# The last row blocks of a matmul with RMS norm: a square for VectorE, a product and scalings for GpSimd

## The chip, the cores and the metric

The kernel runs on one core of a Trainium2 chip. A core has five engines with a queue each: TensorE (PE in the profile), which multiplies matrices into PSUM; VectorE (DVE); ScalarE (ACT); GpSimd (POOL); and SyncE (SP), which here issues the output DMAs. The time is the device time of one execution in microseconds, the median over several runs.

## The reference

```python
def setup_inputs():
    m, k, n = 2048, 2048, 2048
...
def reference(a, b, gamma, eps):
    x = np.matmul(a, b)
    rms = np.sqrt(np.mean(x ** 2, axis=-1, keepdims=True) + eps)
    return (gamma * x / rms).astype(np.float32)
```

Each row of the product is divided by its root mean square over 2048 columns, and multiplied by gamma column by column. All arrays are float32.

## The kernel before

The 2048 rows are done in 16 row blocks of 128 rows, and the columns in four chunks of 512 (`CH`). After a first part that multiplies plainly, row blocks go in pairs (`ra`, `rb`), and each pair of row blocks with each half of the columns is one 2x2 block product. It is computed with seven products instead of eight, in the manner of Strassen and Winograd (`do(n, m)` runs product m of segment n); for some segments the same is done once more on a larger scale (`step`). Partial results lie in PSUM banks (`B1`, `B2`, `B3`, `B7`, `tbank`) and in SBUF tiles `x11`, `x12`, `x21`, `x22`; the helper `add` (L101) joins them on VectorE, and ScalarE copies banks.

Behind each row block come the norm and the output. ScalarE squares a piece and sums it along the row into one column of `msq` (`square_of`, L272, whose squared values go to a junk tile `sq`). A ScalarE root (`root`, L288) of the sums, with the rest of the sum as bias, gives the root mean square, VectorE's reciprocal (L293) gives the row's factor, and the rows are multiplied by it and by gamma and written out by DMAs that SyncE issues. The junk tile comes from a pool with a single buffer (`sq_pool`, bufs=1), and every square asks that pool for its tile anew.

The order of the work on each engine is the order of the program text; nothing reorders it (`manual_schedule`). Waits between engines follow from which tile an operation reads or writes. SyncE's queue also runs in program order: a DMA that waits for its tile holds up those behind it.

The change lies in `last_group`, which finishes row blocks 14 (`ra`) and 15 (`rb`), at the end of the kernel. What matters there, in order of the text:

- `r_a`, the factor of row block 14, is ready. Its four chunks are scaled: `left` by ScalarE (`by_r`, L754), `mid` by GpSimd (L820), `x11[1]` by VectorE (L822; this chunk was multiplied by gamma earlier), `x12[1]` by VectorE with factor and gamma at once (`scaled_gamma`, L750). Three DMAs take them out (L819, L821, L827).
- In between, VectorE adds `x21[1]` to the two half banks (`half`) and to `x22[1]`, which is the last chunk but one of row block 15 to be complete.
- `do(n, 4)` completes `b2[0]`, chunk 0 of row block 15. ScalarE squares `b2[0]` and `x22[1]`; VectorE multiplies chunk 0 by gamma into `xb` and sums what is known of the row's squares (`pre_b`, L832).
- TensorE ends with eight matmuls on each of two half banks of 256 columns (L839), which are chunk 2 of row block 15. ScalarE squares each half (L842). Behind the first, VectorE adds its sum to the rest (`part`) and multiplies `x22[1]` by gamma into `chunk[3]`.
- Root and reciprocal give `r_b`. VectorE scales chunk 0 (L848), and a 256 KB DMA takes it out (L849); ScalarE scales chunks 1 and 3, which lie in the tile `wide`, VectorE the two halves of chunk 2 with gamma, and a DMA of 768 KB takes out the three chunks (L854).

Of the kernel before, what the change touches and what calls it, by code (L numbers as in the profile page):

```python
# [8 lines left out]
FP32 = mybir.dt.float32  # L9
BF16 = mybir.dt.bfloat16  # L10
# [3 lines left out]
ALU = mybir.AluOpType  # L14
# [3 lines left out]
def kernel(  # L18
# [13 lines left out]
    nc = tc.nc  # L32
    P = 128
# [6 lines left out]
    CH = 512  # L40
# [12 lines left out]
    sq_pool = ctx.enter_context(tc.tile_pool(name="sq_pool", bufs=1))  # L53
# [4 lines left out]
    inv_sqrt_n = 1.0 / float(N) ** 0.5  # L58
# [41 lines left out]
    def add(out, in0, in1, op=ALU.add):  # L100
        nc.vector.tensor_tensor(out=out, in0=in0, in1=in1, op=op)  # L101
# [104 lines left out]
    msq = {}  # L206
# [53 lines left out]
    def x_tile(mb, h):  # L260
        if (mb, h) not in x_half:
            x_half[mb, h] = x_slot[slot_of[mb, h]]
        return x_half[mb, h]

    def x_chunk(mb, c):
        return x_tile(mb, c // 2)[:, (c % 2) * CH:(c % 2 + 1) * CH]

    def square_of(mb, src):
        c = n_sq[mb]
        n_sq[mb] += 1  # L270
        sq = sq_pool.tile([P, 2 * CH], BF16, name="sq")
        nc.scalar.activation(out=sq[:, 0:src.shape[-1]], in_=src, func=ACTF.Square,  # L272
                             scale=inv_sqrt_n, accum_out=msq[mb][:, c:c + 1])

    def square_half(mb, h):
        square_of(mb, x_tile(mb, h))
# [4 lines left out]
    def take_pre(mb):  # L281

        pre_of[mb] = stat_pool.tile([P, 1], FP32, name="pre")
        add(pre_of[mb], msq[mb][:, 0:1], msq[mb][:, 1:2])
# [11 lines left out]
    def square_right(mb):  # L296

        square_half(mb, 1)
        rms_of[mb] = root(msq[mb][:, 2:3], pre_of.pop(mb))

    def rows(mb, lo, hi):
        return out[mb * P:(mb + 1) * P, lo:hi]
# [207 lines left out]
    x11, x12, x21, x22 = (x_chunk(r, c) for r in (r2, r3) for c in (2, 3))  # L510
# [45 lines left out]
    def chunks(n):  # L556
        g, j = halves[n]
        return [x_chunk(2 * g + r, 2 * j + c) for r in range(2) for c in range(2)]

    def do(n, m, copies=True):  # L560

        if n >= len(halves) or n < 0:
            return
        g, j = halves[n]
        b1, b2, b3 = B1[n % 2], B2[n % 2], B3[n % 2]
        if g >= G2:
            b1 = b2
        product(g, j, m, {1: b1, 2: b1, 3: b3, 4: b2, 5: b3, 6: b2, 7: B7}[m],
                start=m in (1, 7))
        if m == 1 and g >= G2:  # L570
            nc.scalar.copy(out=chunks(n)[0], in_=b2)
        elif m == 1:
            nc.scalar.copy(out=b2, in_=b1)  # L573
        elif m == 6:
            nc.scalar.copy(out=b3, in_=b2)  # L575
        elif m == 7 and copies:
            nc.scalar.copy(out=chunks(n)[2], in_=B7)  # L577
# [44 lines left out]
    def first_sums(n):  # L622

        return [chunks(m)[0] for m in (n - 2, n - 1, n, n + 1)]
# [115 lines left out]
    def last_group():  # L740
        n = len(halves) - 2
        g = NG - 1
        ra, rb = 2 * g, 2 * g + 1
        x11, x12, x21, x22 = zip(chunks(n), chunks(n + 1))
        xa, xb = x_tile(ra, 0), x_tile(rb, 0)
        gam = [gamma_sb[:, c * CH:(c + 1) * CH] for c in range(NCH)]
        gam_left = gamma_sb[:, 0:HALF]

        def scaled_gamma(x, src, r, gamma_of_x):
            nc.vector.scalar_tensor_tensor(out=x, in0=src, scalar=r, in1=gamma_of_x,  # L750
                                           op0=ALU.mult, op1=ALU.mult)

        def by_r(x, r):
            nc.scalar.activation(out=x, in_=x, func=ACTF.Copy, scale=r)  # L754

        b2, b3 = [B2[(n + j) % 2] for j in range(2)], [B3[(n + j) % 2] for j in range(2)]
        x00, x01 = first_sums(n)[0:2]
        do(n, 6)
        step(g - 1, 1, X2)
        nc.scalar.copy(out=W2, in_=X2)  # L760
        square_right(rb - 2)
        do(n - 1, 3)
        step(g - 1, 2, W2)
        step(g - 1, 6, X2)
        nc.scalar.copy(out=Y2, in_=X2)
        finish(rb - 2)
        take(n - 1, 12)
        add(x00, W2, x00)
        do(n + 1, 1)
        step(g - 1, 5, Y2)  # L770
        step(g - 1, 7, W2)
        step(g - 1, 4, X2)
        square_half(ra - 2, 0)
        add(x11[1], Y2, x11[1])
        a_sums(g, (4,))
        add(x11[0], W2, x11[0])
        add(x11[1], W2, x11[1])
        take_pre(ra - 2)
        square_of(ra, x11[1])
        do(n, 5)  # L780
        nc.scalar.copy(out=x22[0], in_=b3[0])
        add(x11[0], X2, x11[0])
        step(g - 1, 3, Y2)
        add(x01, Y2, x01)
        square_right(ra - 2)
        do(n + 1, 6)
        finish(ra - 2)
        do(n, 7)
        add(x22[0], x21[0], x22[0])
        add(b2[0], b2[0], x21[0])  # L790
        square_of(rb, x22[0])
        add(x11[1], x11[1], gam[2], ALU.mult)
        do(n + 1, 5)
        nc.scalar.copy(out=x22[1], in_=b3[1])
        wide = a_pool.tile([P, K], FP32, name="a32")
        chunk = [wide[:, c * CH:(c + 1) * CH] for c in range(NCH)]
        add(chunk[1], x22[0], gam[1], ALU.mult)
        pre_b = stat_pool.tile([P, 1], FP32, name="part")
        add(pre_b, msq[rb][:, 0:1], msq[rb][:, 1:2])
        do(n, 3)  # L800
        take(n, 12)
        square_half(ra, 0)
        pre_a = stat_pool.tile([P, 1], FP32, name="pre")
        nc.vector.tensor_scalar(out=pre_a, in0=msq[ra][:, 0:1], scalar1=msq[ra][:, 1:2],
                                scalar2=msq[ra][:, 2:3], op0=ALU.add, op1=ALU.add)
        add(xa, xa, gam_left, ALU.mult)
        do(n + 1, 3)
        take(n + 1, 12)
        square_of(ra, x12[1])
        rms_a = root(msq[ra][:, 3:4], pre_a)  # L810
        r_a = inverse(rms_a)
        other = X2
        product(g, 1, 7, other)
        nc.scalar.copy(out=x21[1], in_=other)
        halves2 = [slice(0, CH // 2), slice(CH // 2, CH)]
        half = [bank[:, 0:CH // 2] for bank in (B1[1], b3[0])]
        left, mid = xa[:, 0:CH], xa[:, CH:]
        by_r(left, r_a)
        nc.sync.dma_start(out=rows(ra, 0, CH), in_=left)  # L819
        nc.gpsimd.tensor_scalar_mul(out=mid, in0=mid, scalar1=r_a)  # L820
        nc.sync.dma_start(out=rows(ra, CH, HALF), in_=mid)  # L821
        nc.vector.tensor_scalar_mul(out=x11[1], in0=x11[1], scalar1=r_a)  # L822
        for bank, col in zip(half, halves2):
            add(bank, b2[1][:, col], x21[1][:, col])
        add(x22[1], x21[1], x22[1])
        scaled_gamma(x12[1], x12[1], r_a, gam[3])
        nc.sync.dma_start(out=rows(ra, HALF, N), in_=x_tile(ra, 1))  # L827
        do(n, 4)
        square_of(rb, b2[0])
        square_of(rb, x22[1])  # L830
        add(xb[:, 0:CH], b2[0], gam[0], ALU.mult)
        nc.vector.tensor_scalar(out=pre_b, in0=pre_b, scalar1=msq[rb][:, 2:3],  # L832
                                scalar2=msq[rb][:, 3:4], op0=ALU.add, op1=ALU.add)

        half_sq = stat_pool.tile([P, 2], FP32, name="n2")
        part = stat_pool.tile([P, 1], FP32, name="part")
        for h, (bank, col) in enumerate(zip(half, halves2)):
            for kp in range(KP):
                nc.tensor.matmul(bank, quarter(g, 1, 1)[:, kp, :], sums[1][:, 2, kp, col],  # L839
                                 start=False, stop=(kp == KP - 1), skip_group_check=True)  # L840
            sq = sq_pool.tile([P, 2 * CH], BF16, name="sq")
            nc.scalar.activation(out=sq[:, 0:CH // 2], in_=bank, func=ACTF.Square,  # L842
                                 scale=inv_sqrt_n, accum_out=half_sq[:, h:h + 1])
            if h == 0:
                add(part, half_sq[:, 0:1], pre_b)
                add(chunk[3], x22[1], gam[3], ALU.mult)
        r_b = inverse(root(half_sq[:, 1:2], part))
        nc.vector.tensor_scalar_mul(out=xb[:, 0:CH], in0=xb[:, 0:CH], scalar1=r_b)  # L848
        nc.sync.dma_start(out=rows(rb, 0, CH), in_=xb[:, 0:CH])  # L849
        for c in (1, 3):  # L850
            by_r(chunk[c], r_b)
        for bank, col in zip(half, halves2):
            scaled_gamma(chunk[2][:, col], bank, r_b, gam[2][:, col])
        nc.sync.dma_start(out=rows(rb, CH, N), in_=wide[:, CH:])  # L854

    first_segment()
# [37 lines left out]
```

## Time and profile before

| | |
|---|---|
| median of 3 runs | 219.91 us (219.65 to 221.15) |
| the profiled execution's own time | 219.88 us |
| its span, first to last instruction | 218.1 us |
| TensorE matmul busy | 207.6 us (95%), granted clock 0.991 |
| VectorE busy | 161.9 us (74%) |
| ScalarE busy | 113.6 us (52%) |
| GpSimd busy | 36.8 us (17%), of it one computation in the last 50 us |
| SyncE: output DMAs | 32 |

In the profile a line is that of the kernel, L12 being line 12; where a helper such as `add` records every operation, all of them show the helper's line, and the tile names tell them apart. Lines of a timeline give the start in us from the span's start, the duration, the engine, the line, the operation, its output and inputs with their shapes, and in brackets how long the engine was idle before it and what released it. SPq is SyncE's queue of DMAs. Ends of matmuls are modelled, and durations on GpSimd are rough.

### The profile page before, as it was taken

The page shows a single profiled execution, that of the slowest core. Times are in us where ns is not written, and L with a number is a line of the kernel's source. Part 1 is how long each engine was busy: PE and PEld are TensorE (multiplying, and loading weights), DVE is VectorE, ACT ScalarE, POOL GpSimd, SP SyncE. Part 2 cuts the span into 40 slices and gives each one's busy share as a digit, 9 for nine tenths or more (in the row PEclk, how much of TensorE's full clock was granted, in tenths as well). Part 3 has the DMA queues.
Part 4 walks back from the last instruction along what each step waited for, and adds up shares of the span by engine and source line. Part 5 has one row for each costly group of instructions (what it writes and reads, how often), then busy time and mean ns, then how long its engine had stood idle before and what let it go on. Part 6 is the DMA issues. An engine that isn't in the chain of part 4 may idle for free.

```text
span 218.1 us, 2969 instructions
## 1 busy us (share of the span) xinstructions
PE 207.6 (95%) x1004; PEld 97.1 (45%) x1024; DVE 161.9 (74%) x327; ACT 113.6 (52%) x225; POOL 36.8 (17%) x73
## 2 busy tenths in 40 slices
PE   7899999999999999999999999999999999999970
PEld 3444544444455444444444444444444444444440
DVE  1128769999999974989985899399856984485781
ACT  2110002900598565889726962594728951555782
POOL 7544444334001000300021001100101000000030
PEclk9999999999999999999999999999999999999996
DMA  7999999999949888599774995497595993040454
GB/s 153 171 201 207 203 206 209 212 207 221 408 171 377 304 228 238 150 345 283 237 227 168 345 277 100 183 243 241 126 273 215 316 256 72 0 192 3 192 187 198
DMA packets 37039, 46.60 MB, mean 214 GB/s; under 512 B 22560, under 2 KB 26656, under 8 KB 35744
## 3 DMA queue, kind: packets, MB, share of 16 engines
q0 software_dynamic: 10608, 23.86, 45.3%
q1 hardware_dynamic: 26144, 22.29, 34.8%
q10 hardware_dynamic: 272, 0.26, 0.3%
q8 instruction: 8, 0.13, 0.2%
q14 instruction: 7, 0.06, 0.1%
HBM read 34.60 MB, written 16.78 MB: 236 GB/s over the span
## 4 chain that ended last, share of the span: by engine, by line
PE 80%; DMA 6%; ACT 6%; DVE 4%; issue 2%; POOL 1%; ACTq 0%; another core or an unknown queue 0%; SPq 0%; POOLq 0%
PE acc L358 53%; PE acc L406 16%; PE acc L397 3%; DMA early<-in_a_dram 3%; DMA out_dram<-x 3%; ACT sq L272 2%; PE tbank L397 2%; PE tbank L432 2%; DVE x L311 2%; PE tbank L182 2%; PE tbank L358 1%; DVE x L101 1%; ACT acc L573 0%; PE tbank L195 0%; POOL b L115 0%
## 5 line engine op out<-in xcount | busy, mean ns | idle before, releaser
L358 PEld LDWEIGHTS <-s 128*128 128x128 f16 (+1 forms) x312 | 30.4, 98 | 37.5 <-DVE s L335 1.1
L272 ACT ACTIVATE sq<-x 128x1024 bf16<-128x1024 f32 (+1 forms) x33 | 33.2, 1005 | 25.0 <-DVE x L101 21.1
L406 PE MATMUL acc<-b,head_at 128*128 128x512 bf16 x171 | 42.3, 379 | 0.6 <-DMA b<-in_b_dram 0.4
L311 DVE SCALAR_TENSOR_TENSOR x<-x,r,gamma_sb 128x1024 f32<-128x1024 f32 x28 | 34.9, 1282 | 0.5
L358 PE MATMUL acc<-b,head_at 128*128 128x512 bf16 x133 | 33.6, 379 | 0.2
L101 DVE TENSOR_TENSOR x<-acc,x 128x512 f32<-128x512 f32 x33 | 22.2, 687 | 10.7 <-PE acc L397 4.7
L358 PEld LDWEIGHTS <-head_at 128*128 128x128 f16 (+1 forms) x184 | 17.9, 98 | 21.0
L358 PE MATMUL acc<-b,at_even 128*128 128x512 bf16 x110 | 26.2, 379 | 0.2
L406 PEld LDWEIGHTS <-head_at 128*128 128x128 bf16 x176 | 16.9, 97 | 19.7 <-issue 0.7
L358 PE MATMUL acc<-early,s 128*128 128x512 bf16 x102 | 25.4, 379 | 0.2
L358 PE MATMUL acc<-b,s 128*128 128x512 bf16 x100 | 24.3, 379 | 0.2
L358 PEld LDWEIGHTS <-at_even 128*128 128x128 f16 x160 | 15.7, 98 | 18.9
L224 ACT ACTIVATE sq<-a 128x1024 bf16<-128x1024 f32 x22 | 23.3, 1058 | 0.5
L358 PE MATMUL acc<-t_left,s 128*128 128x512 bf16 x95 | 22.5, 379 | 0.1
L115 POOL DMA_DIRECT2D b<-in_b_dram x32 | 17.2, 541 | 20.5 <-DMA b<-in_b_dram 14.1
L442 ACT COPY x<-acc 128x512 f32<-128x512 f32 x7 | 4.1, 580 | 25.6 <-PE acc L406 25.6
L575 ACT COPY acc<-acc 128x512 f32<-128x512 f32 x12 | 6.9, 575 | 10.6 <-PE acc L358 10.6
L293 DVE RECIPROCAL r<-rms 128x1 f32<-128x1 f32 x16 | 2.6, 160 | 12.1 <-ACT rms L288 12.0
L187 DVE COPY head_at<-tbank 128x1024 bf16<-128x1024 bf16 x7 | 4.8, 692 | 8.3 <-PE tbank L182 8.3
L820 POOL TENSOR_SCALAR x<-x,r 128x512 f32<-128x512 f32 x1 | 1.9, 1855 | 42.0 <-DVE r L293 42.0
L101 DVE TENSOR_TENSOR x<-tbank,x 128x512 f32<-128x512 f32 x9 | 6.2, 689 | 3.6 <-PE tbank L432 3.6
L577 ACT COPY x<-acc 128x512 f32<-128x512 f32 x10 | 5.8, 585 | 5.0 <-PE acc L358 5.0
(133 smaller groups left out, 244.7 us busy)
## 6 DMA issues: line engine op xcount, KB each, us to landing
out_dram<-x SPq DMA_DIRECT2D x29, 512.0 KB, 3.7
a<-in_a_dram POOLq DMA_DIRECT2D x9, 1024.0 KB, 5.9
b<-in_b_dram POOLq DMA_DIRECT2D x32, 256.0 KB, 9.9
a<-in_a_dram POOLq DMA_DIRECT2D x4, 512.0 KB, 9.8
early<-in_a_dram POOLq DMA_DIRECT2D x7, 256.0 KB, 10.0
gamma_sb<-in_gamma_dram POOLq DMA_DIRECT2D x2, 512.0 KB, 9.9
head_at<-in_a_dram POOLq DMA_DIRECT2D x1, 1024.0 KB, 8.9
out_dram<-x SPq DMA_DIRECT2D x3, 256.0 KB, 2.6
```

The lines of the kernel that those rows point to most:

```text
L101: nc.vector.tensor_tensor(out=out, in0=in0, in1=in1, op=op)
L115: nc.gpsimd.dma_start(out=raw[j][kp][:, t, :], in_=b[lo:lo + P, j * HALF:(j + 1) * HALF])
L182: nc.tensor.matmul(view[:, t, r, :], ah(kp)[:, r, t * P:(t + 1) * P], identity, is_transpose=True, start=(t == 0 and r == 0), stop=(t == 1 ...
L187: nc.vector.tensor_copy(out=head_at[:, 2 * kp:2 * kp + 2, :, :], in_=view)
L224: nc.scalar.activation(out=junk, in_=a32[mb][:, h * HALF:(h + 1) * HALF], func=ACTF.Square, scale=2.0 ** -8, accum_out=n2[:, h:h + 1])
L272: nc.scalar.activation(out=sq[:, 0:src.shape[-1]], in_=src, func=ACTF.Square, scale=inv_sqrt_n, accum_out=msq[mb][:, c:c + 1])
L311: nc.vector.scalar_tensor_tensor(out=x, in0=x, scalar=inverse_of[mb], in1=gamma_sb[:, h * HALF:(h + 1) * HALF], op0=ALU.mult, op1=ALU.mult)
L358: nc.tensor.matmul(bank, lhsT[:, kp, :], rhs, start=(start and kp == 0), stop=(kp == KP - 1), skip_group_check=not start)
L397: nc.tensor.matmul(bank, lhsT[:, k, :], rhs, start=(m in (1, 7) and k == 0), stop=(k == KQ - 1), skip_group_check=m not in (1, 7))
L406: nc.tensor.matmul(bank, head_at[:, kt, r, :], head_rhs(c, kt), start=(kt == 0), stop=(kt == KT - 1))
L575: nc.scalar.copy(out=b3, in_=b2)
L577: nc.scalar.copy(out=chunks(n)[2], in_=B7)
```

## The change

All of it is in `last_group`. A helper `by_r_pool` scales a tile on GpSimd by the row's factor and, as a second multiplication in the same instruction, by 1.0. For row block 14, `mid` uses this form, and `x11[1]` moves from VectorE to GpSimd. `x22[1]` is squared and summed by VectorE in one instruction (`tensor_tensor_reduce`, with `pre_b` as the initial value of the sum and a junk tile from the same pool, seen as 512 float32), ahead of the scaling of `x12[1]`; the ScalarE square and the sum L832 go. GpSimd takes the product of `x22[1]` with gamma, ahead of the last matmuls in the text. VectorE's sum behind the first half square adds three columns at once, and the product of chunk 0 with gamma follows it. At the end ScalarE scales chunk 0 and the first half of chunk 3, GpSimd chunk 1 and the second half of chunk 3, and VectorE the two halves of chunk 2, as before.

```diff
+        def by_r_pool(x, r):
+            nc.gpsimd.tensor_scalar(out=x, in0=x, scalar1=r, scalar2=1.0,
+                                    op0=ALU.mult, op1=ALU.mult)
+
         by_r(left, r_a)
         nc.sync.dma_start(out=rows(ra, 0, CH), in_=left)
-        nc.gpsimd.tensor_scalar_mul(out=mid, in0=mid, scalar1=r_a)
+        by_r_pool(mid, r_a)
         nc.sync.dma_start(out=rows(ra, CH, HALF), in_=mid)
-        nc.vector.tensor_scalar_mul(out=x11[1], in0=x11[1], scalar1=r_a)
+        by_r_pool(x11[1], r_a)
         for bank, col in zip(half, halves2):
             add(bank, b2[1][:, col], x21[1][:, col])
         add(x22[1], x21[1], x22[1])
+        sq = sq_pool.tile([P, 2 * CH], BF16, name="sq")
+        nc.vector.tensor_tensor_reduce(out=sq.bitcast(FP32), in0=x22[1], in1=x22[1],
+                                       scale=inv_sqrt_n * inv_sqrt_n, scalar=pre_b,
+                                       op0=ALU.mult, op1=ALU.add, accum_out=msq[rb][:, 3:4])
+        nc.gpsimd.tensor_tensor(out=chunk[3], in0=x22[1], in1=gam[3], op=ALU.mult)
         scaled_gamma(x12[1], x12[1], r_a, gam[3])
         nc.sync.dma_start(out=rows(ra, HALF, N), in_=x_tile(ra, 1))
         do(n, 4)
         square_of(rb, b2[0])
-        square_of(rb, x22[1])
-        add(xb[:, 0:CH], b2[0], gam[0], ALU.mult)
-        nc.vector.tensor_scalar(out=pre_b, in0=pre_b, scalar1=msq[rb][:, 2:3],
-                                scalar2=msq[rb][:, 3:4], op0=ALU.add, op1=ALU.add)
...
             if h == 0:
-                add(part, half_sq[:, 0:1], pre_b)
-                add(chunk[3], x22[1], gam[3], ALU.mult)
+                nc.vector.tensor_scalar(out=part, in0=half_sq[:, 0:1], scalar1=msq[rb][:, 2:3],
+                                        scalar2=msq[rb][:, 3:4], op0=ALU.add, op1=ALU.add)
+                add(xb[:, 0:CH], b2[0], gam[0], ALU.mult)
         r_b = inverse(root(half_sq[:, 1:2], part))
-        nc.vector.tensor_scalar_mul(out=xb[:, 0:CH], in0=xb[:, 0:CH], scalar1=r_b)
+        by_r(xb[:, 0:CH], r_b)
         nc.sync.dma_start(out=rows(rb, 0, CH), in_=xb[:, 0:CH])
-        for c in (1, 3):
-            by_r(chunk[c], r_b)
+        by_r_pool(chunk[1], r_b)
         for bank, col in zip(half, halves2):
             scaled_gamma(chunk[2][:, col], bank, r_b, gam[2][:, col])
+        by_r(chunk[3][:, halves2[0]], r_b)
+        by_r_pool(chunk[3][:, halves2[1]], r_b)
         nc.sync.dma_start(out=rows(rb, CH, N), in_=wide[:, CH:])
```

## The prediction

> **What bounds the kernel now.** I read the page first: TensorE is busy 95% of the span and carries 80% of the chain of waits. None of its work is touched, so only what lies behind its last matmul (211.12 us) can change the time, and that is 7.0 of 218.1 us. Then I read the end of the chain of waits in order of time (start, us, what):
>
> ```profile
> 209.41 0.30 ACT sq L272
> ...
> 210.13 0.17 ACT sq L272
> ...
> 210.88 0.48 ACT sq L842 x2
> 211.37 0.02 issue
> 211.39 0.21 ACT sq L842
> ...
> 211.90 0.30 ACT rms L288
> 212.20 0.02 issue
> 212.23 0.17 DVE r L293
> ...
> 212.47 0.72 ACT a L754
> 213.20 0.61 ACTq L889
> ```
>
> The end does not hang on the last matmuls: ScalarE is behind them. It has four squares in a row (L272 on b2[0] and on x22[1], then the two half banks of L842), then the root, VectorE's reciprocal, and two scalings. From 209.41 its starts step by 0.72 (b2[0]), 0.75 (x22[1]), 0.51, 0.51 and 0.33 to the reciprocal at 212.23. The second half bank is squared at 211.39, 0.27 after the matmuls end; that slack is all that a shorter ScalarE queue can win.
>
> Third, the timeline of VectorE, GpSimd and SyncE for the same stretch (start, us, engine, line):
>
> ```profile
> 207.86 0.49 DVE L822 TENSOR_SCALAR x<-x,r 128x512 f32<-128x512 f32 x1
> 207.92 1.85 POOL L820 TENSOR_SCALAR x<-x,r 128x512 f32<-128x512 f32 x1 [42.02 <-DVE r L293]
> 208.30 0.76 DVE L101 TENSOR_TENSOR acc<-acc,x 128x256 f32<-128x256 f32 x2
> 208.97 0.68 DVE L101 TENSOR_TENSOR x<-x 128x512 f32<-128x512 f32 x1
> 209.57 0.75 DVE L750 SCALAR_TENSOR_TENSOR x<-x,r,gamma_sb 128x512 f32<-128x512 f32 x1
> ...
> 212.94 0.33 SPq L849 DMA_DIRECT2D out_dram<-x  x1
> 213.83 0.33 SPq L854 DMA_DIRECT2D out_dram<-a  x1
> ```
>
> GpSimd has one operation here, and it takes 1.85 us where VectorE takes 0.49 for the same shape. The last two output DMAs (256 KB, then 768 KB) are issued at 212.94 and 213.83.
>
> Fourth, the stretches of 0.25 us (last number: GB/s moved; I looked at all from 209 on):
>
> ```profile
> 213.50:213.75 0.25, 0.00 (x0) 0.00 (x0) 0.20 (x1) 0.25 (x1) 0.00 (x0) 1.00 0.00 0
> 213.75:214.00 0.25, 0.00 (x0) 0.00 (x0) 0.00 (x0) 0.06 (x1) 0.00 (x0) 1.00 0.84 319
> ...
> 216.25:216.50 0.25, 0.00 (x0) 0.00 (x0) 0.00 (x0) 0.00 (x0) 0.00 (x0) 0.50 0.99 393
> 216.50:216.75 0.25, 0.00 (x0) 0.00 (x0) 0.00 (x0) 0.00 (x0) 0.00 (x0) 0.50 0.04 0
> ```
>
> The 1 MB of the last rows flows from 213.75 to 216.5, without a gap, at 303 to 418 GB/s: from 0.81 after the **first** of the two issues. So the 256 KB issue matters as much as the last one: the end is the later of (first issue + 0.81 + 1 MB, 2.75 us here) and (last issue + about 0.65 + 768 KB at 400 GB/s, 1.95 us), and then 1.6 us of closing. An earlier last issue alone wins nothing.
>
> **The change, part by part.**
>
> *Square of x22[1] from ScalarE to VectorE.* ScalarE loses its 0.75 step. VectorE gets a product with a sum. No such row exists; the same engine's product of two 128x512 f32 takes 0.68, the scalar_tensor_tensor form 0.75, and ScalarE's readout of a sum 0.19. Bounds 0.68 and 0.94, I take 0.85, nearer to the form with most operands. It starts where L750 starts now, 209.57 to 209.6, and ends near 210.45. Here the change **adds a wait**: both engines put their junk into the same one-buffer tile sq. ScalarE's next square (b2[0], now at 209.41) writes that tile too, so it must wait for VectorE: 210.45, +1.04. Queued behind it are both half squares and the root. New starts: half squares 211.17 and 211.68, root 212.19, done for the reciprocal at 212.52. Net: +1.04 - 0.75 = +0.29 where a gain of up to 0.27 was to be had.
>
> *VectorE's order.* The L822 scaling goes to GpSimd (0.49), but the bank adds behind it wait for ScalarE's copy of x21 (L814, to 208.27) anyway: nothing won. The x12 scaling moves behind the new square, to about 210.3 to 211.05, so the DMA of L827 issues near 211.07 instead of 210.35. SyncE's queue holds nothing due before 212.9, and the DMA engines are idle from 213.0 to 213.75, so the 0.7 us are hidden; without that gap they would be paid. The two small sums become one (L832's form, 0.27), and the xb product (0.68) takes the place that the chunk[3] product had behind it. Part needs the first half square's sum, 211.67; the product runs from 211.87 to 212.55, so the reciprocal starts at 212.55 against 212.23: +0.32.
>
> *xb scaled by ScalarE, not VectorE.* L754's form takes 0.72, L848 took 0.49. ScalarE started 0.24 after the reciprocal's start: 212.79 to 213.51, and the 256 KB issue comes at 213.53 against 212.94: +0.59. By the fourth view this alone moves the end by 0.59, or by about 0.5 if the dip to 303 GB/s between the two transfers closes.
>
> *GpSimd's scalings.* Now mid, x11[1], the chunk[3] product, chunk[1], and half of chunk[3]. The two-multiplication form has no row. The nearest is L820, 1.855, its only run. On this engine first runs are long; the L146 casts of a single column (timeline of GpSimd):
>
> ```profile
> 87.58 1.25 POOL L146 CAST pace<-head_at 128x1 f32<-128x1 f16 x1 [19.55 <-DMA head_at<-a]
> ...
> 156.50 0.35 POOL L146 CAST pace<-at_even 128x1 f32<-128x1 f16 x1 [15.48 <-DMA at_even<-a]
> ```
>
> That is 0.90 less by the last one. L820 less 0.90 is 0.95; I take 1.0 for 512 columns and 0.55 for 256. The ends are 0.49 (VectorE's speed) and 1.855, and twice that, 3.7, if each multiplication costs what one does now. The product on GpSimd: 0.68 (VectorE) to 1.86, up to 2.8 with a first run's 0.90; I take 1.86, the engine's own row. Then mid 207.92 to 208.92, x11[1] to 209.92, product to 211.8, all before the factor comes. Chunk[1] starts 0.26 after the reciprocal's start, as L820 did: 212.81 to 213.81, the half to 214.36, last issue 214.4. ScalarE's half of chunk[3] is done by 213.9, VectorE's two halves of chunk[2] (0.87) by 213.8: GpSimd ends last, but 214.4 + 0.65 + 1.95 = 217.0 is no later than 213.53 + 0.81 + 2.75 = 217.1.
>
> **Sum.** The data ends at 217.1 against 216.5: +0.6. The profiled execution took 219.88 for a span of 218.1, 0.03 under the median of the three runs (219.91), so the forecast is 219.88 + 0.6 = **220.5 us**.
>
> [...] The add at 208.97 reads two tiles of SBUF beside GpSimd's L820 and takes its usual 0.68, starting at once. [...]
>
> **Rivals.**
> - *GpSimd sets the end* (27%). Its scaling really takes 1.855, first run or not. Then mid ends 209.78, x11[1] 211.63, the product at 212.3 to 213.5, chunk[1] (from 212.81 at the earliest) at 214.67 to 215.35, the half at 215.6 to 216.3: last issue 1.8 to 2.5 later, 221.7 to 222.4, and up to 223.3 with a slow first product. It decides from about 1.1 us per 512 columns on. For it: the only row of this operation. Against: first runs of this engine are long. Dearer still, two multiplications at 3.7 a piece (6%): the queue alone ends past 219, above 226.
> - *No wait on the junk tile, or a hidden one* (15%), not slower. Squares at 209.41, 210.25 and 211.15, reciprocal held by the xb product to 212.1, the xb issue at 213.05 to 213.1, 0.13 late; with the dip closed the data ends at 216.5: 219.9. For it: ScalarE sits idle for 0.52 before 209.41. Against: one buffer, two engines that write it.
> - *The sum of squares is slower or quicker than 0.85* only moves the forecast by 0.1 either way.
>
> **How the numbers follow.** Forecast 50%, 220.5 (220.2 to 221.0); GpSimd as bound 27%; its double 6%; no wait 15%; the rest, 2%, is a gain that I can't name. The range reaches from the no-wait case less the 0.26 between the lowest run and the median, 219.6, to 222.6, which leaves out the double and the slowest products. Faster by over 1% (2.2 us, about what a measurement of this kernel can tell from no change) would need a last issue before 211.7, 0.6 after the last matmul, where the square, root and reciprocal alone take 1.3: 2%. Slower by over 1% means over 222.1: the upper half of GpSimd's case and the double, 22%. Within: 76%.
>
> **What would show it.** In the profile after: ScalarE's square of b2[0] starting about 210.4 and released by VectorE; the reciprocal near 212.55; the 256 KB issue near 213.5; GpSimd's 512-column scalings near 1.0, the last issue near 214.4. A square at 209.41 breaks the first step, scalings of 0.5 or of 1.8 the fourth; a GpSimd operation that stretches VectorE's two-input rows beyond 0.75 means that the row at 208.97 misled me.

## The result and the profile after

The changed kernel takes 222.12 us (median of 22 runs, 221.08 to 223.93) against 220.09 us for the kernel before in the same comparison (22 runs, 219.44 to 222.44). The ratio is 1.0088 with a 95% interval of 1.0063 to 1.0112: 1.9 us slower, 1.4 to 2.5 by the interval (the medians alone differ by 2.0). The profiled execution has a span of 220.3 us.

The last reciprocal before the end, r_a's, stands at 207.66 in the profile before and at 208.22 in the one after (VectorE's timelines):

```profile
207.66 0.16 DVE L293 RECIPROCAL r<-rms 128x1 f32<-128x1 f32 x1 [0.37 <-ACT rms L288]
```

```profile
208.22 0.16 DVE L293 RECIPROCAL r<-rms 128x1 f32<-128x1 f32 x1 [0.37 <-ACT rms L288]
```

Up to there the two programs are the same, and over the twelve profiles of this study that point lies anywhere from 207.3 to 211.3, so the 0.56 says nothing about the change. All times below that are called *relative* therefore count from the start of r_a's reciprocal; from there on, instructions that the programs have in common repeat to about 0.01 us. They are read from the traces in ns, and differences are formed before rounding, so a difference can deviate by 0.01 from that of the rounded figures. From r_a to the end it is 10.43 before and 12.09 after: **1.66 us** that the tail accounts for.

First, the timeline of VectorE in the changed kernel (start, us, engine, line, operation, in brackets the idle time before it and its releaser):

```profile
209.54 0.85 DVE L101 TENSOR_TENSOR x<-x 128x512 f32<-128x512 f32 x1
210.43 0.75 DVE L832 CUSTOM_DVE_ANT_0 sq<-x,part 128x512 f32<-128x512 f32 x1
211.11 0.08 DVE L832 DVE_READ_ACCUMULATOR2_ANT msq<- 128x1 f32 x1
211.11 1.75 DVE L750 SCALAR_TENSOR_TENSOR x<-x,r,gamma_sb 128x512 f32<-128x512 f32 x1
212.78 0.26 DVE L851 TENSOR_SCALAR part<-n,msq 128x1 f32<-128x1 f32 x1
212.96 0.67 DVE L101 TENSOR_TENSOR x<-acc,gamma_sb 128x512 f32<-128x512 f32 x1
213.56 0.15 DVE L293 RECIPROCAL r<-rms 128x1 f32<-128x1 f32 x1
```

The new square is the first L832 row: 0.75, and 0.08 in the second for the readout of its sum, which begins before the square ends; the two together take 0.76. The row to look at is L750, the scaling of x12: 1.75 where it took 0.75 before. Behind it wait the sum L851, the product of chunk 0 and r_b's reciprocal, at 213.56, relative 5.34 (4.57 before).

Second, ScalarE and then GpSimd:

```profile
211.28 0.60 ACT L272 ACTIVATE sq<-acc 128x512 bf16<-128x512 f32 x1 [1.83 <-DVE msq L832]
...
213.13 0.29 ACT L288 ACTIVATE rms<-n,part 128x1 f32<-128x1 f32 x1
```

```profile
208.49 1.36 POOL L820 TENSOR_SCALAR x<-x,r 128x512 f32<-128x512 f32 x2 [42.14 <-DVE r L293]
210.53 1.77 POOL L835 TENSOR_TENSOR a<-x,gamma_sb 128x512 f32<-128x512 f32 x1 [0.68 <-POOL x L820]
213.80 1.15 POOL L820 TENSOR_SCALAR a<-a,r 128x512 f32<-128x512 f32 x2 [1.50 <-DVE r L293]
```

ScalarE does wait for VectorE's square before it squares b2[0], 1.83 us, as forecast. GpSimd scales two tiles of 512 columns in 1.36 us, 0.68 each. Its product L835 runs from 210.53 to 212.30, and that is where VectorE's L750 is stuck: VectorE ends it at 212.85, 0.55 after GpSimd is through.

Third, the end of the chain of waits (start, us, what):

```profile
210.53 1.77 POOL a L835
212.30 1.45 issue
213.75 0.75 POOLq L897
214.50 0.45 POOL a L820
```

Before, this chain ended in ScalarE's scaling L754. Now it ends in GpSimd's last scaling, 214.95, although the span goes on to 220.3 and although the last output DMA, which SyncE issues at 214.99, has landed by 218.7. L897 is the end of the program, not a line of the kernel's work. The closing instructions show why it stands there. These are GpSimd's drains at the program's end, before and after (count, durations in ns min/median/max, first and last start in us):

```profile
L889 POOLq DRAIN  x3: 46/93/6499, 207.9 to 217.8; - x3
```

```profile
L897 POOLq DRAIN  x3: 46/93/5782, 213.8 to 220.0; - x3
```

The first drain of each is the long one. Before, it lasts from 207.86 to 214.36, to 4.58 us past the end of GpSimd's only computation here, 209.78. After, from 213.75 to 219.53: again 4.58 us past the last computation, at 214.95. In both traces the program's closing handshake goes through GpSimd: the other engines count up one semaphore at their drains (SyncE at 217.32 before), GpSimd's wait for it ends at 217.35, it counts up another at 217.43, and the others' waits for that one end from 217.47 to 217.53. SyncE had seen all outputs landed and was ready at 217.32 before (relative 9.66), and there GpSimd had been free for 3 us; after, SyncE is ready at 218.85 (10.63), and GpSimd answers at 219.58 (11.35). 0.7 us of the loss lies there, behind the last byte.

### The profile page after: what moved, and what is told of

Its sections match the earlier page's. It is cut to its first block, busy times and chain, and to the rows that moved or that the text cites. A ratio compares the mean times of both kernels' runs of the same rounds, so it can differ in the third digit from the quotient of the medians.

```text
span 220.3 us, 2971 instructions
## 1 busy us (share of the span) xinstructions
PE 208.2 (94%) x1004; PEld 97.4 (44%) x1024; DVE 162.1 (74%) x325; ACT 112.7 (51%) x223; POOL 38.1 (17%) x77
## 4 chain that ended last, share of the span: by engine, by line
PE 79%; DMA 6%; ACT 4%; DVE 4%; issue 2%; POOL 2%; POOLq 0%; ACTq 0%; SPq 0%
PE acc L358 52%; PE acc L406 16%; PE acc L397 3%; DMA early<-in_a_dram 3%; DMA out_dram<-x 3%; PE tbank L397 2%; ACT sq L272 2%; PE tbank L432 2%; DVE x L311 2%; PE tbank L182 2%; POOL a L835 1%; PE tbank L358 1%; DVE x L101 1%; ACT acc L573 0%; PE tbank L195 0%
## 5 line engine op out<-in xcount | busy, mean ns | idle before, releaser
L272 ACT ACTIVATE sq<-x 128x1024 bf16<-128x1024 f32 (+1 forms) x32 | 32.5, 1017 | 24.4 <-DVE x L101 20.6
L820 POOL TENSOR_SCALAR x<-x,r 128x512 f32<-128x512 f32 x2 | 1.4, 684 | 42.1 <-DVE r L293 42.1
```

## The experiments

Two theories stood against each other for each half of the loss. For the late end: **D**, that GpSimd's drain is a cost of late GpSimd work, against **R**, that only the landing of the data counts. For the late r_b: **J**, the wait on the shared junk tile, as the prediction had it, against **P**, that GpSimd's product holds VectorE up. The table has all runs; times in the first five columns are relative to r_a's reciprocal.

```
                  r_b    first   SyncE   GpSimd   to the   ratio to before
                         issue   ready   drained  end      (95% interval)
before            4.57   5.28    9.66    6.70     10.43    1
after             5.34   6.26    10.63   11.31    12.09    1.0088 (1.0063-1.0112)
a_old_tail        5.33   6.03    10.43    8.66    11.19    1.0048 (1.0016-1.0079)
b_new_tail        4.57   5.52    9.89    10.62    11.40    1.0050 (1.0014-1.0086)
b_late_touch      4.57   5.28    9.68    11.05    11.83    1.0055 (1.0025-1.0085)
a_junk_port       4.39   5.34    9.72    10.38    11.16    1.0054 (1.0019-1.0088)
a_own_junk        5.33   6.27    10.64   11.31    12.10    one run
a_free_port       5.12   6.07    10.45   11.11    11.89    one run
a_one_mult        5.26   6.20    11.46   12.57    13.35    1.0153 (1.0098-1.0208)
b_split           4.57   5.15    10.26    6.70    11.03    1.0043 (1.0010-1.0076)
a_three_out       4.40   5.11    9.50     6.22    10.26    0.9997 (0.9963-1.0031)
a_vector_product  4.93   5.63    10.02    6.21    10.80    1.0018 (0.9984-1.0051)
```

The end of each program is the later of "SyncE ready" and "GpSimd drained" plus about 0.77, in every row.

**Late GpSimd work, three ways.** `a_old_tail` takes it out of the changed kernel:

```diff
-        by_r(xb[:, 0:CH], r_b)
+        nc.vector.tensor_scalar_mul(out=xb[:, 0:CH], in0=xb[:, 0:CH], scalar1=r_b)
...
-        by_r_pool(chunk[1], r_b)
+        for c in (1, 3):
+            by_r(chunk[c], r_b)
...
-        by_r(chunk[3][:, halves2[0]], r_b)
-        by_r_pool(chunk[3][:, halves2[1]], r_b)
```

> The changed kernel with the scalings behind r_b as they were before (VectorE chunk 0, ScalarE chunks 1 and 3); all else as changed. In the changed kernel's profile GpSimd's closing drain ends 4.58 us after its last computation, at 219.53, and the closing handshake that SyncE reached at 218.85 waits for it until 219.58. Theory D (late GpSimd work costs this drain): GpSimd's last computation is now the gamma product, which ends about 4.1 after r_a's reciprocal, so the drain ends under the output and costs nothing: 0.73 of the drain and 0.22 of the quicker first scaling go, about 1.0 us faster than the changed kernel and 0.8 slower than before (r_b is still 0.77 late), a ratio near 1.004. Rival R (the drain is a number without effect, all that counts is when the last data lands): 0.2 faster than the changed kernel, a ratio near 1.008.

Measured: ratio 1.0048; the stretch to the end 11.19, 0.90 under the changed kernel, with r_b as late as there. This profiled execution lost some 3 us ahead of r_a, which the relative times leave out. Theory D held, R did not.

`b_new_tail` makes the reverse edit in the kernel before: the changed scalings behind r_b, with the two-multiplication helper, and nothing else.

> The kernel before with the changed scalings behind r_b alone (ScalarE chunk 0 and half of chunk 3, GpSimd chunk 1 and the other half). Theory D: r_b comes as before, 4.57 us after r_a's reciprocal; the data ends at most 0.2 later; GpSimd's last scaling ends about 1.15 + 0.25 behind r_b's reciprocal, its drain 4.58 after that, 0.8 to 0.9 behind SyncE: 0.9 slower than before, ratio 1.004. Rival R: 0 to 0.2 slower, ratio 1.000 to 1.001. Rival S (GpSimd's scalings themselves are the bound, 1.0 us or more per 512 columns): 0.5 or more slower by a later last DMA issue.

Measured: ratio 1.0050, r_b at 4.57, stretch 11.40, which is 0.97 more. The first issue comes 0.23 later than before and SyncE is ready 0.23 later; the other 0.74 is GpSimd's drain, which ends at 10.62. The scalings themselves took 0.69 and 0.47, so S falls.

`b_late_touch` asks for the drain alone: one column, read late, written where nobody looks.

```diff
+        nc.gpsimd.tensor_copy(out=pace, in_=chunk[3][:, 0:1])
         nc.sync.dma_start(out=rows(rb, CH, N), in_=wide[:, CH:])
```

> The kernel before, with one GpSimd copy of a single column (128x1) added that reads chunk 3 after ScalarE has scaled it and writes a tile that nobody reads. Theory D: the copy ends near 6.4 after r_a's reciprocal, the drain 4.58 later, where SyncE is done at 9.66: the span grows by 1.2 to 1.4 us, ratio 1.0055 to 1.0065, while the last DMA issue and the last landing stay where they were. Rival R: nothing, ratio 1.000. If the drain depends on the size of the operation, between the two.

Measured: ratio 1.0055, stretch 11.83, 1.40 more, with both output issues at the same relative times as before (5.28 and 6.18) and the last landing at 9.47 against 9.46. Its timeline of GpSimd, and of SyncE's queue the waits (what waited for what: us in total, times, longest):

```profile
209.04 1.85 POOL L820 TENSOR_SCALAR x<-x,r 128x512 f32<-128x512 f32 x1 [42.02 <-DVE r L293]
215.05 0.18 POOL L854 COPY pace<-a 128x1 f32<-128x1 f32 x1 [4.16 <-ACT a L754]
```

```profile
SPq L890 <- PEq L890: 2.0, 2, 1.6
SPq L890 <- DMA out_dram<-a: 1.6, 1, 1.6
```

A copy of 0.18 us costs 1.4 us of the profiled stretch, and 1.2 us by the ratio (0.6 to 1.9 by its interval). In the kernel before the same first line reads 0.7, 2, 0.5. The wait is put down to TensorE's queue, which had long been done: it is the handshake that GpSimd had not yet joined, with its drain ended at 11.05 and SyncE ready at 9.68. The drain ended 4.58 after this copy, as after 256 or 512 columns in the other kernels: in these runs that time did not change with the size of the operation. What the drain does in that time, no run shows.

**What holds r_b.** `a_junk_port` takes away both suspects at once:

```diff
+        nc.gpsimd.tensor_copy(out=chunk[3], in_=x22[0])
...
-        sq = sq_pool.tile([P, 2 * CH], BF16, name="sq")
-        nc.vector.tensor_tensor_reduce(out=sq.bitcast(FP32), in0=x22[1], in1=x22[1],
+        nc.vector.tensor_tensor_reduce(out=a16_half.bitcast(FP32), in0=x22[1], in1=x22[1],
...
-        nc.gpsimd.tensor_tensor(out=chunk[3], in0=x22[1], in1=gam[3], op=ALU.mult)
```

> The changed kernel with two waits taken away at once: VectorE's square writes its junk to a tile of its own (the idle half-row tile a16_half) instead of the shared one, and GpSimd's product of x22[1] with gamma is replaced by a copy of x22[0] into chunk 3 some 5 us earlier, so that nothing of GpSimd lies beside VectorE's square and its scaling of x12; chunk 3 of the last row block is then a copy of chunk 1 without its product with gamma. If these two account for the late r_b: ScalarE squares b2[0] about 1.75 after r_a's reciprocal (3.06 changed), the scaling of x12 takes 0.75 (1.75 changed), and r_b's reciprocal comes 4.3 to 4.4 after r_a's (4.57 before, 5.34 changed). Total 0.9 to 1.0 us under the changed kernel, still 0.9 over before, since the drain stays: ratio about 1.004. If something else holds r_b (VectorE's own queue is too long), r_b stays over 4.8.

Measured: r_b at 4.39, 0.18 **earlier** than before; b2[0] is squared at 1.75 and x12 scaled in 0.75 (VectorE's lines):

```profile
211.83 0.75 DVE L750 SCALAR_TENSOR_TENSOR x<-x,r,gamma_sb 128x512 f32<-128x512 f32 x1
...
213.34 0.16 DVE L293 RECIPROCAL r<-rms 128x1 f32<-128x1 f32 x1
```

So the freed square does help ScalarE, and the two waits account for all of r_b's lateness. The 0.18 is not free, though: this kernel leaves out a product that VectorE had before. The total is still 1.0054: GpSimd's drain ends at 10.38, 0.66 behind SyncE. The next two kernels each have one half of this edit: `a_own_junk` the lines on the junk tile, `a_free_port` the other two.

> The changed kernel with VectorE's square writing its junk to a tile of its own (a16_half); GpSimd's product stays where it is. Theory P (VectorE is itself held: GpSimd's product keeps it from scaling x12, and the sum L851 queues behind that scaling): ScalarE squares b2[0] at 1.75 after r_a's reciprocal instead of 3.06, but x12's scaling still takes 1.75, the sum still starts near 4.55, and r_b's reciprocal comes 5.2 to 5.35 after r_a's, as in the changed kernel (5.34). Rival J (the wait on the shared junk tile alone makes r_b late, as the prediction has it): r_b at 4.5 to 4.9.

Measured: r_b at 5.33, 0.001 earlier, and one time of 222.52. The lines of ScalarE:

```profile
210.40 0.60 ACT L272 ACTIVATE sq<-acc 128x512 bf16<-128x512 f32 x1 [0.52 <-PE acc L358]
...
212.21 0.38 ACT L847 ACTIVATE sq<-acc 128x256 bf16<-128x256 f32 x1 [0.40 <-PE acc L844]
...
213.56 0.30 ACT L288 ACTIVATE rms<-n,part 128x1 f32<-128x1 f32 x1 [0.87 <-DVE part L850]
```

The squares are early now and released by TensorE, but the root then waits 0.87 us for VectorE's sum, which is queued behind the 1.75 of L750. J falls as the cause of the lateness in the changed kernel; P holds.

> The changed kernel with the shared junk tile, and GpSimd's product replaced by an earlier copy of x22[0] into chunk 3 (that chunk of the last row block is then not its product with gamma). Theory P: x12's scaling takes 0.75, the sum starts at 4.28 behind the first half square, the product of chunk 0 ends near 5.13, r_b at 5.15: 0.2 earlier only, since the junk tile still holds ScalarE to 3.06. If GpSimd's product alone were the cause: r_b near 4.4. Together with the run before: each wait alone hides the other.

Measured: r_b at 5.12, one time of 221.34. Now VectorE waits for ScalarE (its lines):

```profile
210.55 0.75 DVE L750 SCALAR_TENSOR_TENSOR x<-x,r,gamma_sb 128x512 f32<-128x512 f32 x1
211.96 0.27 DVE L851 TENSOR_SCALAR part<-n,msq 128x1 f32<-128x1 f32 x1 [0.66 <-ACT sq L848]
```

Of the 0.94 us between 5.34 and 4.39, taking away the product alone wins 0.21 and the junk tile alone nothing: each wait hides the other, and either is enough to keep r_b over 5.1. GpSimd's product and L750 read the same piece of gamma, but VectorE was held without a shared tile too: its add beside GpSimd's scaling of `x11[1]` shares none with it and still took 0.85 instead of 0.68, in the changed kernel, `a_junk_port`, `a_own_junk` and `a_free_port`.

**The form of GpSimd's scalings.** `a_one_mult` writes them as before:

```diff
-            nc.gpsimd.tensor_scalar(out=x, in0=x, scalar1=r, scalar2=1.0,
-                                    op0=ALU.mult, op1=ALU.mult)
+            nc.gpsimd.tensor_scalar_mul(out=x, in0=x, scalar1=r)
```

> The changed kernel with GpSimd's scalings in the form of before, one multiplication. Theory F (the form makes the duration): each scaling of 512 columns takes 1.4 to 1.85 in every run, the third as the first; mid and x11 end at 3.1 to 4.0 after r_a's reciprocal, chunk 1 and the half chunk 3 take 2.1 to 2.8 together behind r_b, and the total is 1.0 to 2.0 us over the changed kernel, ratio 1.013 to 1.018. Rival W (only an engine's first run of an operation is long, as the prediction took it): the first is 1.4 to 1.85, the others 0.7 to 0.95, total within 0.3 of the changed kernel, ratio near 1.009.

Measured: ratio 1.0153, stretch 13.35. GpSimd's timeline:

```profile
207.85 3.16 POOL L820 TENSOR_SCALAR x<-x,r 128x512 f32<-128x512 f32 x2 [42.11 <-DVE r L293]
210.98 1.49 POOL L834 TENSOR_TENSOR a<-x,gamma_sb 128x512 f32<-128x512 f32 x1
213.10 2.46 POOL L820 TENSOR_SCALAR a<-a,r 128x512 f32<-128x512 f32 x2 [0.63 <-DVE r L293]
```

Two scalings of 512 columns take 3.16, the third, after r_b, 1.57, and the half one 0.93; the first is no longer than the third. The form decides, F: 1.57 with one multiplication, 0.68 with two. The 1.85 of the kernel before is 0.29 longer; there VectorE's own scaling L822 lay beside it, which this kernel doesn't have. No run changes that alone. VectorE's add and square beside the first two scalings:

```profile
208.90 0.68 DVE L101 TENSOR_TENSOR x<-x 128x512 f32<-128x512 f32 x1
209.62 1.06 DVE L831 CUSTOM_DVE_ANT_0 sq<-x,part 128x512 f32<-128x512 f32 x1
```

**A version that beats both?** `b_split` tries the fourth view of the prediction on the kernel before: let the last 1 MB start to flow earlier.

```diff
+        for col in halves2:
+            nc.vector.tensor_scalar_mul(out=xb[:, col], in0=xb[:, col], scalar1=r_b)
+            nc.sync.dma_start(out=rows(rb, col.start, col.stop), in_=xb[:, col])
+        by_r(chunk[1], r_b)
+        nc.sync.dma_start(out=rows(rb, CH, HALF), in_=chunk[1])
+        by_r(chunk[3], r_b)
...
-        nc.sync.dma_start(out=rows(rb, CH, N), in_=wide[:, CH:])
+        nc.sync.dma_start(out=rows(rb, HALF, N), in_=wide[:, HALF:])
```

> The kernel before, its last 1 MB sent in four DMAs instead of two: VectorE scales chunk 0 in two halves with a DMA behind each, chunk 1 has a DMA of its own, chunks 2 and 3 the last. If the flow of the last 1 MB starts 0.81 behind the first issue and stays full, the first issue comes 0.2 earlier (5.05 against 5.28 after r_a's reciprocal), the data ends 0.25 to 0.4 earlier, and the span with it: 0.3 us faster than before, ratio 0.9985, below what the times can tell, but to be seen in the stretch from r_a to the end (10.43 before). If smaller DMAs cost more per byte or issuing four takes too long, no gain or a loss of up to 0.3.

Measured: slower, ratio 1.0043. The first issue came only 0.13 earlier, the four issues follow each other by 0.42 to 0.50, the last stands at 6.55 instead of 6.18, and the last landing at 9.70 instead of 9.46. SyncE was ready 0.56 after that landing, against 0.20 before: it waited for its DMAs one after the other at 0.06 each, and seven such waits stood behind the one that ended last. Whether the smaller DMAs or the later last issue put the landing back, this run doesn't separate.

`a_three_out` closes the account: own junk tile, no product beside VectorE, old scalings.

> The changed kernel with all three costs taken out: a junk tile of its own for VectorE's square, no product of GpSimd beside VectorE (chunk 3 of the last row block is an early copy of x22[0] instead of its product with gamma), and the scalings behind r_b as before. If the terms add up, r_b comes 4.39 after r_a's reciprocal, the first output issue 0.18 earlier than before (5.10), and the stretch from r_a's reciprocal to the end is 10.2 to 10.3 (10.43 before, 12.09 changed): all that ScalarE's freed square can bring, 0.2 us, with one product less. If a further cost hides, it is over 10.4.

Measured: 10.26, r_b at 4.40, ratio 0.9997. The terms add up, and what the freed square is worth is 0.16 us with one product less, which the times can't tell from nothing. `a_vector_product` is the complete kernel nearest to it:

```diff
                 add(xb[:, 0:CH], b2[0], gam[0], ALU.mult)
+                add(chunk[3], x22[1], gam[3], ALU.mult)
```

> A complete kernel: the changed one with a junk tile of its own for the square, the scalings behind r_b as before, and the product of x22[1] with gamma on VectorE as before, behind chunk 0's. If VectorE's queue is full once it has the square (0.67 more from start to start), the second product ends near 5.05 after r_a's reciprocal and r_b comes at 5.05 to 5.1, not 4.39: the stretch to the end is 10.9 to 11.0, 0.5 over before, ratio about 1.002. If VectorE has room, r_b at 4.4 to 4.6 and the time is that of before.

Measured: r_b at 4.93, stretch 10.80, ratio 1.0018, an interval that holds 1. That is 0.12 earlier than expected, but the expected mechanism: ScalarE's root ends at 4.36, and r_b's reciprocal stands behind the product on VectorE. In this order VectorE has no room for the square unless something leaves its queue; other orders, such as the product behind the reciprocal, were not tried. None of these beats the kernel before.

## Why the prediction was right, and where it was not

The time lies in the range and within the 1% that had 76%, though barely: the interval of the ratio reaches 1.0112, and the time itself, 222.12, stands at the 222.1 that was named as the edge. It moved to the slower side, as the forecast of +0.6 did. But +0.6 is a third of what came: 1.66 in the tail, 1.9 by the ratio. That the range holds the time is in part luck: its upper part, above 221.0, was there for slow scalings on GpSimd, which turned out quick, and it was filled by two losses that the forecast had at nothing. (Half of 27% and 6% also make some 20%, not the 22% given for slower by over 1%.) By its own steps:

- *The wait on the junk tile.* Forecast for 210.45, relative 2.79; measured 3.06, released by VectorE. The wait is real, but it does not set r_b in this kernel: `a_own_junk` shows that taking it away alone brings nothing. Where it is the only one of the two left, in `a_free_port`, r_b is 0.55 late, against the 0.32 forecast from it.
- *The square on VectorE.* 0.85 was taken; square and readout together took 0.76.
- *The add at 208.97.* This step failed. The add had run undisturbed beside GpSimd's L820, 0.68, and from that row the product was costed at nothing for VectorE. Measured: L750 at 1.75, r_b 0.77 late instead of 0.32. In these rows the instruction that started second ended only after the first was through: VectorE's new square ended at 211.18 and GpSimd's product 1.12 later; the product ended at 212.30 and L750 0.55 later. Even the add grew, from 0.68 to 0.85: GpSimd's second scaling ended at 209.85, the add 0.54 after it. The row at 208.97 stood beside the one-multiplication form: in `a_one_mult`, which has that form, the add beside it takes 0.68 again, and the square beside its second scaling takes 1.06 but ends 0.34 ahead of that scaling. Why that form lets the add pass was not tried.
- *The price of the product on GpSimd.* 1.86 was taken, 1.77 stands in the row, but 0.65 of it had passed when VectorE's square ended. From the end of VectorE's instruction it took 1.12, in this kernel and in `a_one_mult`, where it ended at relative 4.89 and VectorE's L750 at 3.77.
- *GpSimd's scalings at 1.0 per 512.* 0.68 measured. The reason given, that a first run is long, is wrong; the form is the reason. The step's conclusion, that below 1.1 the scalings do not set the last landing, held, and with it the reading that the first of the two last issues decides. In the ten profiles whose second issue follows the first by 0.50 to 0.90, the last landing comes 4.17 to 4.20 after the first issue; in `a_one_mult`, where it follows by 1.81, 5.05 after. The 0.65 taken from the last issue to its bytes was the author's estimate, and no run shows it; from that issue to its landing it is 3.29 before and 3.67 after. The DMA of x12 left 2.00 later than before, not 0.7, and that too was hidden.
- *Chunk 0 on ScalarE.* +0.27 forecast (0.59 less r_b's 0.32), 0.21 measured (0.98 less 0.77), 0.23 in `b_new_tail`.
- *"Then 1.6 us of closing."* This step failed as well. The closing was taken as fixed, and no step of the prediction counted GpSimd's drain. It costs 0.69 here and about 0.74 in `b_new_tail`, and `b_late_touch` shows it with nothing else changed. It was to be seen before: a drain of 6.5 us that began at 207.9 stood among the closing instructions.

In sum: 0.77 for r_b and 0.21 for ScalarE's slower scaling make the first issue 0.98 later, and SyncE is ready 0.97 later; from there GpSimd answered after 0.03 before and after 0.72 now. 0.97 and 0.69 are the 1.66. The rival "GpSimd sets the end" named 221.7 to 222.4, and the time fell there, but not by its mechanism: the last DMA issue came 0.6 later than before, not 1.8 to 2.5.

## What to carry to other kernels

The end of this program is set by GpSimd's closing as well as by the last byte: look up when GpSimd last computes and how long after that its drain ends (4.58 us in these runs), and keep its work further than that from the end. Work given to GpSimd was not free for VectorE here: beside GpSimd's product and its two-multiplication scaling, a VectorE instruction that reads two tiles of SBUF and started second (L750, the add) ended 0.54 to 0.55 after GpSimd's. When two waits stand side by side in front of one step, removing either shows little (0.21 and nothing here, 0.94 together), so an experiment has to remove both, and then each.

## What the runs showed of the hardware

- GpSimd's closing drain ended 4.58 us after its last computation in all twelve profiles, after 0.18 us of copy (`b_late_touch`) as after 1.77 us of product (`a_old_tail`).
- On GpSimd a multiplication of 128x512 float32 by a per-row factor took 1.57 us written with one multiplication (`a_one_mult`; 1.85 in the kernel before) and 0.68 to 0.69 with a second one by 1.0. Durations on GpSimd are rough, but from start to start of two in a row it was 1.56 and 0.68.
- VectorE's product with a sum, 128x512 float32, took 0.75, and 0.08 for the readout, 0.76 in all; in the kernel before ScalarE's square of the same piece took 0.63 and 0.19, 0.72 in all.
- VectorE's scalings of chunk 2, which read one of their two tiles from PSUM, took 0.48 and 0.47 beside GpSimd's two-multiplication scaling, and 0.48 each without it in the kernel before: they were not held.
- SyncE waited for its finished output DMAs one by one at 0.06 us each, and in `b_split`, where the DMA that landed last was waited for early in that row, it was ready 0.36 us later behind that landing than before.
- SyncE's queue issued in program order: in the changed kernel GpSimd had scaled `mid` by 209.18, and its DMA (L826) left at 209.91, behind that of `left` (L824, 209.48), which waited for ScalarE.
